# Router logits from the residual's sums, with norm and modulation folded into the router's weights and two rows, and the first pair's rows gathered one token tile at a time

## The chip, the core and the metric

The kernel runs on one core of a Trainium2 chip. The time is that of one execution on the device in microseconds (us); the median of 3 runs stands for it. The rows below come from one profiled execution of the same program. In them PE is TensorE's matmuls, PEld its weight loads, DVE is VectorE, ACT is ScalarE, POOL is GpSimd, SP is the engine whose queue issues nearly all transfers.

## The reference, cut to what matters

One transformer block on 256 tokens of width 1024: a mixer (attention, gated linear attention, pooling), then a mixture of 32 experts of which each token takes 4.

```python
h = x * (1.0 + scale1) + shift1
y = hybrid_mixer(h, ...)                                   # ends in  concat @ w_out
x = layer_norm(ALPHA * x + (1.0 + gate1) * y, ln1_g, ln1_b)
h = x * (1.0 + scale2) + shift2                            # six rows of cond @ w_ada + b_ada
logits = h @ w_router + b_router                           # 1024 -> 32
top_logit, top_e = lax.top_k(logits, 4)
gate = softmax(top_logit)
# each expert: clamped_swiglu(h_rows @ w_gate_up[e] + b) @ w_down[e] + b, weighted by gate, summed per token
x = layer_norm(ALPHA * x + (1.0 + gate2) * y, ln2_g, ln2_b)
```

With r the residual's sum before the first norm, mu and s its mean and inverse deviation of a token, and h = n * hA + hB for the normed row n = (r - mu) * s (hA = ln1_g * (1 + scale2), hB = ln1_b * (1 + scale2) + shift2), the logits are s * (r @ (hA * W)) - mu * s * (sum of hA * W) + (sum of hB * W) + b_router. That is the identity that the change uses.

## The kernel before

The tokens stand in two tiles (t = 0, 1) of 128. The program is a straight list of operations; a scheduler at build time sets the order on each engine, and each engine then runs its own list strictly in order, waiting on semaphores.

**The mixer.** Attention, the linear attention and the pool fill `oT`, the mixer's output with the features on the partitions, in eight blocks k. For attention each head's probabilities `sc` are transposed on PE (`ppT`, lines 560 and 562), copied by ACT to `pT` and multiplied into `po`; DVE copies `po` to `oT` (line 569). Then `py[t][n]` = oT @ w_out is accumulated in four banks, blocks 0, 1, 2, 6, 7 first and the linear attention's blocks 3, 4, 5 at the end.

**Rows of w_ada.** scale2 and shift2 are needed as columns (`m2`): DVE multiplies eight row blocks by cond and adds them up (`accm`, line 546, two sums j = 0, 1 of eight steps), PE adds over the partitions (`pcol`, eight small matmuls for each j), and DVE makes `hA` and `hB` (lines 550 to 553). The rows of gate1 (`acc`) and gate2 (`g2p`) are added up the same way (lines 622 and 624), from tiles `adag`.

**Norm and router, for each t.** DVE makes the residual in place in `n` (the tile n1), its statistics and the inverse deviation; ACT and DVE write the normed row (lines 667 and 668). PE transposes it (`ph`), ACT and DVE modulate it into `h2T` (lines 680 and 682), PE makes the logits on 32 partitions (`plg`), DVE adds the bias, PE turns them back (`plt`). Top-4, the experts' one-hot sum `msel` and the slot numbers `posm` follow (lines 691 to 702).

**The experts.** They are taken in 16 pairs, each expert with 64 slots. `dispatch` builds a one-hot matrix `pp` from `posm`, PE gathers the pair's rows with it (`pxg`), DVE and ACT modulate them into `xg`. `gate_up` multiplies them with four weight tiles `g` of 2 MB, `down` with two tiles `d` of 2 MB.

**The ring.** All large weights go through a ring of five buffers of 2 MB, and from the experts on through three more (`ring2`) that lie where the mixer's tiles were. `adag`, `wo` (two tiles of w_out; wo1 holds the blocks 7, 3, 4, 5) and the first expert tiles `g` follow each other in it. SP issues each load when the tile that held the buffer has had its last reader; its queue is in order too, so a load that waits holds back those behind it. The fifth expert tile takes the buffer of wo1, whose last reader is the last matmul of `py`; the three of `ring2` stand behind it.

Of the kernel before, what the change touches and what calls it, by code (L numbers as in the profile page):

```python
# [112 lines left out]
def block_kernel(ctx: ExitStack, tc, x, w_ada, w_in, gla_w_a2, pool_w, w_out, w_router, w_gate_up, b_gate_up,  # L113
# [57 lines left out]
    def layer_norm_stats(st, pool, name):  # L171
# [4 lines left out]
        return mv[:, 0:1], rs  # L176


    with tc.tile_pool(name="early", bufs=1) as ea, tc.tile_pool(name="late", bufs=1, side="right") as la_, \
# [189 lines left out]
        z2 = la_.tile([P, TT, ZN - O_GV], F32, name="z2")  # L369
# [44 lines left out]
        gaT = ea.tile([RANK, S], F32, name="gaT")  # L414
# [177 lines left out]
        o_gla = la_.tile([P, TT, GVW], F32, name="o_gla")  # L592
# [60 lines left out]
        oh = []  # L653
        for t in range(TT):
            st6 = la_.tile([P, 2, 6], F32, tag="st", name=f"st{t}")
            for n in range(2):
# [414 lines left out]
```

## Time and profile before

| | us |
|---|---|
| median of 3 runs (1127.11 to 1131.95) | 1128.25 |
| the profiled execution, as timed | 1129.8 |
| its span, first to last instruction | 1128.0 |
| PE busy (matmuls; their ends are modelled) | 1035.4 |
| DVE, ACT, POOL busy | 318.7, 98.8, 41.5 |

A busy time is a sum over stages with different limits; it doesn't say which engine sets the end. The transfers of 449.49 MB took 398 GB/s over the span. The stages are the mixer (to about 150 us), norm and router (150 to 187 us) and the experts (187 us to the end).

### The profile page before, as it was taken

The page shows a single profiled execution, that of the slowest core. Times are in us where ns is not written, and L with a number is a line of the kernel's source. Part 1 is how long each engine was busy: PE and PEld are TensorE (multiplying, and loading weights), DVE is VectorE, ACT ScalarE, POOL GpSimd, SP SyncE. Part 2 cuts the span into 40 slices and gives each one's busy share as a digit, 9 for nine tenths or more (in the row PEclk, how much of TensorE's full clock was granted, in tenths as well). Part 3 has the DMA queues.
Part 4 walks back from the last instruction along what each step waited for, and adds up shares of the span by engine and source line. Part 5 has one row for each costly group of instructions (what it writes and reads, how often), then busy time and mean ns, then how long its engine had stood idle before and what let it go on. Part 6 is the DMA issues. An engine that isn't in the chain of part 4 may idle for free.

```text
span 1128.0 us, 11046 instructions
## 1 busy us (share of the span) xinstructions
PE 1035.4 (92%) x4734; PEld 436.9 (39%) x4735; DVE 318.7 (28%) x587; ACT 98.8 (9%) x205; POOL 41.5 (4%) x43
## 2 busy tenths in 40 slices
PE   6999998999999999996999999989989898989795
PEld 3656545434333333333344343423333333333231
DVE  1459694322222122211122221213221121211113
ACT  1024112100000000000000000000000000000100
POOL 2270000000000000000000000000000000000000
PEclk9999897999999999998999999999999999999998
DMA  9997499999999999999899999999999999999992
GB/s 324 348 385 283 181 378 373 428 423 428 428 428 427 428 428 428 428 427 423 344 427 428 428 428 426 428 427 428 428 428 427 428 429 427 428 427 428 428 414 92
DMA packets 52998, 449.49 MB, mean 398 GB/s; under 512 B 5056, under 2 KB 18768, under 8 KB 28496
## 3 DMA queue, kind: packets, MB, share of 16 engines
q1 hardware_dynamic: 52320, 447.90, 95.7%
q8 instruction: 39, 0.64, 0.2%
q10 hardware_dynamic: 624, 0.83, 0.2%
q14 instruction: 15, 0.12, 0.0%
HBM read 447.67 MB, written 1.05 MB: 398 GB/s over the span
## 4 chain that ended last, share of the span: by engine, by line
PE 29%; DMA 22%; DVE 1%; issue 1%; ACT 0%; POOL 0%; DVEq 0%; POOLq 0%
DMA d<-in_w_down 22%; PE gu L134 13%; PE py L134 7%; PE pxg L134 4%; PE ya L134 3%; PE pyl L134 1%; PE paT L837 1%; DVE yb L855 0%; DVE aT L839 0%; DVE res L919 0%; ACT n L931 0%; PE pln L134 0%; DVE r L1038 0%; DVE yl L1015 0%; DVE st L1019 0%
## 5 line engine op out<-in xcount | busy, mean ns | idle before, releaser
L134 PE MATMUL gu<-g,xg 128*64 128x512 f32 x2048 | 462.5, 595 | 14.0 <-DMA g<-in_w_gate_up 12.6
L134 PEld LDWEIGHTS gu<-g,xg 128*64 128x64 f32 x2048 | 143.2, 137 | 295.5 <-issue 261.0
L134 PE MATMUL py<-d,aT 128*64 128x512 f32 x992 | 227.1, 600 | 13.8 <-DMA d<-in_w_down 12.5
L825 DVE TENSOR_SCALAR g<-gu 128x512 f32<-128x512 f32 x32 | 22.1, 692 | 410.1 <-PE gu L134 410.1
L134 PEld LDWEIGHTS py<-d,aT 128*64 128x64 f32 x992 | 70.0, 137 | 150.5 <-issue 140.8
L134 PE MATMUL pxg<-pp,n 128*128 128x128 f32 x512 | 77.0, 302 | 14.9 <-DVE aT L839 7.0
L134 PEld LDWEIGHTS pxg<-pp,n 128*128 128x128 f32 x512 | 69.2, 208 | 43.0 <-issue 29.6
L855 DVE TENSOR_TENSOR yb<-py,g2p 64x512 f32<-64x512 f32 x60 | 41.3, 689 | 139.0 <-PE py L134 138.4
L134 PE MATMUL ya<-yb,sg_None 128*128 128x512 f32 x120 | 58.2, 607 | 4.9 <-DVE yb L855 4.8
L829 ACT ACTIVATE s<-g 128x512 f32<-128x512 f32 x32 | 20.2, 630 | 464.4 <-DVE g L825 464.4
L793 DVE TENSOR_SCALAR xg<-pxg,hA,hB 128x128 f32<-128x128 f32 x64 | 25.8, 409 | 99.2 <-PE pxg L134 90.0
L791 ACT ACTIVATE xg<-pxg,hB,hA 128x128 f32<-128x128 f32 x64 | 28.7, 457 | 274.3 <-DVE xg L793 273.6
L134 PE MATMUL pz<-wz,hT 128*128 128x512 f32 (+2 forms) x128 | 52.4, 547 | 0.0
L169 POOL TENSOR_TENSOR rsb<-rtb,half 128x2 f32<-128x2 f32 x1 | 0.7, 701 | 950.9 <-DVE rtb L168 950.9
L839 DVE COPY aT<-paT 128x512 f32<-128x512 f32 x32 | 22.1, 692 | 43.9 <-PE paT L837 43.8
L134 PE MATMUL py<-wo,oT 128*128 128x512 f32 x64 | 30.9, 629 | 0.2 <-ACT oT L642 0.2
L134 PEld LDWEIGHTS ya<-yb,sg_None 128*128 128x128 f32 x120 | 20.4, 189 | 26.9 <-issue 17.4
L134 PEld LDWEIGHTS pz<-wz,hT 128*128 128x128 f32 x128 | 23.4, 190 | 17.3 <-issue 14.3
L837 PEld LDWEIGHTS paT<-kc,l 128*128 128x128 f32 x128 | 18.0, 209 | 25.3 <-DVE l L831 15.4
L837 PE MATMUL paT<-kc,l 128*128 128x128 f32 x128 | 23.7, 308 | 0.0
L831 DVE TENSOR_TENSOR l<-l,s 128x512 f32<-128x512 f32 x32 | 22.1, 691 | 3.4 <-DVE l L830 0.5
L134 PE MATMUL pqk<-hT,wz 128*128 128x256 f32 x96 | 22.2, 381 | 0.7 <-DVE hT L332 0.7
(245 smaller groups left out, 519.1 us busy)
## 6 DMA issues: line engine op xcount, KB each, us to landing
g<-in_w_gate_up SPq DMA_DIRECT2D x128, 2048.0 KB, 30.4
d<-in_w_down SPq DMA_DIRECT2D x62, 2048.0 KB, 30.4
adam<-in_w_ada SPq DMA_DIRECT2D x4, 2048.0 KB, 16.7
adag<-in_w_ada SPq DMA_DIRECT2D x4, 2048.0 KB, 9.0
ada<-in_w_ada SPq DMA_DIRECT2D x6, 1024.0 KB, 11.1
wz<-in_w_in SPq DMA_DIRECT2D x8, 760.0 KB, 9.5
wo<-in_w_out SPq DMA_DIRECT2D x2, 1536.0 KB, 10.0
ada<-in_w_ada SPq DMA_DIRECT2D x4, 512.0 KB, 7.4
```

Of the source, the lines that this page charges most:

```text
L134: T.matmul(o, l, r, start=start, stop=stop, skip_group_check=True, **kw)
L169: G.tensor_tensor(o, t[:, :n], half[:, :n], op=OP.pow)
L791: A.activation(xg[:, k], bs[k // 4][:, k % 4], AF.Identity, bias=hB[:, k:k + 1], scale=hA[:, k:k + 1])
L793: V.tensor_scalar(xg[:, k], bs[k // 4][:, k % 4], hA[:, k:k + 1], hB[:, k:k + 1], op0=OP.mult, op1=OP.add)
L825: V.tensor_scalar(g, gu[:, 0], LIMIT, None, op0=OP.min)
L829: A.activation(s, g, AF.Sigmoid, scale=SW_ALPHA)
L831: V.tensor_mul(l, l, s)
L837: T.transpose(b[:, j], act[:, j::4], ident)
L839: V.tensor_copy(aT, b)
L855: V.tensor_mul(yb[m * CAP:(m + 1) * CAP, n * 512:(n + 1) * 512], b[r], g2p[r, n * 512:(n + 1) * 512])
```

## The change

The router no longer waits for the norm. The router's weights are multiplied by hA and by hB once (`wr2`), summed over the partitions and the eight blocks (`wrs`, PE `prow`) into two rows `rrow`; that code stands right behind hA and hB. In the loop over t each half of the residual is transposed as soon as it is made, copied by ACT to `h2T` unmodulated, and the logits come out on 128 partitions from `h2T` as the stationary operand and `wr2` of 32 columns; one DVE instruction applies the deviation and adds the row. The first pair's one-hot matrix is built and its rows are gathered in the loop, tile by tile (`pxgA`, in two banks that `py` had), and modulated into `xgA`, a buffer that the even pairs then use; the odd ones have the other. Some tiles share space differently: the 4 KB of `xgA` stand in the part of SBUF that lives through the whole program, `gaT` shares with `pm`, `z2` is split, and `o_gla` takes the place of `z_gr`.

```diff
+    xgA = const.tile([P, KT, P], F32, name="xgA")
...
+    def one_hot(pp, pcol, t):
+
+        V.tensor_tensor(pp[:, t], pcol[:, t, :, None].to_broadcast([P, 2, CAP]),
+                        iota1[:, None, :].to_broadcast([P, 2, CAP]), op=OP.is_equal)
+
+    def gathered(bs, pp, t):
+
+        for k in range(KT):
+            mm(bs[k // 4][:, k % 4], twos(n1[:, t], k), pp[:, t].rearrange("p a s -> p (a s)"),
+               t == 0 and k % 4 == 0, t == TT - 1)
+
+    def modulated(xg, bs):
+        for k in range(KT):
+            if k % 2:
+                A.activation(xg[:, k], bs[k // 4][:, k % 4], AF.Identity, bias=hB[:, k:k + 1], scale=hA[:, k:k + 1])
+            else:
+                V.tensor_scalar(xg[:, k], bs[k // 4][:, k % 4], hA[:, k:k + 1], hB[:, k:k + 1], op0=OP.mult, op1=OP.add)
...
+        wr2 = la_.tile([P, 2, KT, NE], F32, tag="qin", name="wr2")
+        for j, h in enumerate((hA, hB)):
+            V.tensor_mul(wr2[:, j], wr, h[:, :, None].to_broadcast([P, KT, NE]))
+        wrs = la_.tile([P, 2, NE], F32, name="wrs")
+        V.tensor_reduce(wrs, wr2.rearrange("p j k e -> p j e k"), axis=AX.X, op=OP.add)
+        b = bank("prow")
+        mm(b[:, 0:2 * NE], ones, wrs.rearrange("p j e -> p (j e)"), True, False)
+        mm(b[:, NE:2 * NE], colv[:, 80:81].to_broadcast([P, P]), kc[:, K_I4:K_I4 + NE], False, True)
+        rrow = la_.tile([P, 2, NE], F32, name="rrow")
+        V.tensor_copy(rrow, b[:, 0:2 * NE].rearrange("p (j e) -> p j e", j=2))
...
                 V.bn_stats(st6[:, n], y)
+                b = bank(f"ph{t}{n}").rearrange("p (j s) -> p j s", j=4)
+                for j in range(4):
+                    T.transpose(b[:, j], twos(xs[:, t], 4 * n + j), ident)
+                A.copy(h2T[:, 4 * n:4 * n + 4, t * P:(t + 1) * P], b)
             mu, rs = layer_norm_stats(st6, la_, f"a{t}")
             nmr = la_.tile([P, 1], F32, tag="nmr", name=f"nmr{t}")
             V.scalar_tensor_tensor(nmr, mu, -1.0, rs, op0=OP.mult, op1=OP.mult)
+            row = la_.tile([P, NE], F32, tag="row", name=f"row{t}")
+            V.scalar_tensor_tensor(row, rrow[:, 0], nmr, rrow[:, 1], op0=OP.mult, op1=OP.add)
+            b = bank(f"plg{t}")
+            for k in range(KT):
+                mm(b[:, 0:NE], h2T[:, k, t * P:(t + 1) * P], wr2[:, 0, k], k == 0, k == KT - 1)
+            V.scalar_tensor_tensor(lg[:, t], b[:, 0:NE], rs, row, op0=OP.mult, op1=OP.add)
...
-            for q in range(2):
-                b = bank(f"ph{t}{q}").rearrange("p (j s) -> p j s", j=4)
-                for j in range(4):
-                    k = 4 * q + j
-                    T.transpose(b[:, j], twos(n1[:, t], k), ident)
-                for j in range(4):
-                    k = 4 * q + j
-                    o = h2T[:, k, t * P:(t + 1) * P]
-                    if j % 2:
-                        A.activation(o, b[:, j], AF.Identity, bias=hB[:, k:k + 1], scale=hA[:, k:k + 1])
-                    else:
-                        V.tensor_scalar(o, b[:, j], hA[:, k:k + 1], hB[:, k:k + 1], op0=OP.mult, op1=OP.add)
-            b = bank(f"plg{t}")
-            for k in range(KT):
-                g = slice(32 * (k // 2), 32 * (k // 2) + 32)
-                mm(b[g, :P], wr[:, k], h2T[:, k, t * P:(t + 1) * P], k % 2 == 0, k % 2 == 1)
-            V.tensor_scalar(lgp[:, t * P:(t + 1) * P], b[:, :P], colv[:, 80:81], None, op0=OP.add)
-            b = bank(f"plt{t}")
-            mm(b[:, 0:NE], lgp[:, t * P:(t + 1) * P], kc[:, K_I4:K_I4 + NE], True, True)
-            V.tensor_copy(lg[:, t], b[:, 0:NE])
...
             V.scalar_tensor_tensor(posm[:, t], b[:, 0:NE], 1.0, msel[:, t], op0=OP.add, op1=OP.mult)
+            one_hot(ppA, posm[:, :, 0:2], t)
+            if t == 0:
+                first = [bank(f"pxgA{q}", "z").rearrange("p (j s) -> p j s", j=4) for q in range(2)]
+            gathered(first, ppA, t)
+        modulated(xgA, first)
...
+        if nm == "0":
+            xg = xgA
+        else:
+            xg = xgA if nm in evens else wk.tile([P, KT, P], F32, tag="xg", name=f"xg{nm}", bufs=1)
+            bs = [mps.tile([P, 4, P], F32, tag="m", name=f"pxg{nm}_{q}") for q in range(2)]
```

The scheduler moves instructions with it; three places are shown. The first is PE's list between the linear attention's transposes and the attention's output, in the program at the end of `pz` (the last part of w_in). Before:

```order
L134 MATMUL pcol_645<-kc,accm_636 128x4 x8
L560 MATMUL ppT_678<-kc,sc_508 128x128
L562 MATMUL ppT_678<-kc,sc_509 128x128 x2
L134 MATMUL po_677<-pT_682,z_397 64x256
...
L134 MATMUL kv_742<-z_398,kout 128x192
L134 MATMUL pcol_664<-kc,accm_655 128x4 x8
L134 MATMUL py_841<-wo_158,oT 128x512
```

And with the change:

```order
L134 MATMUL pcol_647<-kc,accm_638 128x4 x8
L134 MATMUL pcol_666<-kc,accm_657 128x4 x8
L134 MATMUL prow<-wrs,kc 128x64
L134 MATMUL prow<-kc,colv 128x32
L592 MATMUL ppT_690<-kc,sc_510 128x128
L594 MATMUL ppT_690<-kc,sc_511 128x128 x2
L134 MATMUL po_689<-pT_694,z_398 64x256
```

The second `pcol` (of the sum accm with j = 1) stood behind all of the attention's output, and now stands with `prow` ahead of its first transpose. The second place is DVE's list at the same point of the program, from the first result of `pcol` (`m`) on. Before:

```order
L550 TENSOR_TENSOR m_635<-pcol_645,colv 128x8
L546 SCALAR_TENSOR_TENSOR accm_655<-adam_0_154,cond,accm_655 128x1024
L546 SCALAR_TENSOR_TENSOR accm_655<-adam_1_156,cond,accm_655 128x1024
L574 TENSOR_TENSOR sg<-sg,z_398 128x768
L546 SCALAR_TENSOR_TENSOR accm_655<-adam_1_156,cond,accm_655 128x1024
L569 COPY oT<-po_677 128x256
L546 SCALAR_TENSOR_TENSOR accm_655<-adam_1_156,cond,accm_655 128x1024
L569 COPY oT<-po_695 128x256
L546 SCALAR_TENSOR_TENSOR accm_655<-adam_1_156,cond,accm_655 128x1024
```

And with the change (`sg` is the gate of the linear attention, `acc` the sum for gate1):

```order
L569 TENSOR_TENSOR m_637<-pcol_647,colv 128x8
L565 SCALAR_TENSOR_TENSOR accm_657<-adam_0_155,cond,accm_657 128x1024
L565 SCALAR_TENSOR_TENSOR accm_657<-adam_1_157,cond,accm_657 128x1024
L606 TENSOR_TENSOR sg<-sg,z_gr 128x768
L565 SCALAR_TENSOR_TENSOR accm_657<-adam_1_157,cond,accm_657 128x1024
L607 TENSOR_TENSOR sg<-sg,zb 128x768
L565 SCALAR_TENSOR_TENSOR accm_657<-adam_1_157,cond,accm_657 128x1024 x2
L569 TENSOR_TENSOR m_637<-pcol_666,colv 128x8
L570 TENSOR_TENSOR hA<-m_637,colv 128x8
L571 TENSOR_TENSOR hB<-m_637,colv 128x8
L578 TENSOR_TENSOR wr_679<-wr,hA 128x256
```

The copies of `po` moved behind the sums and the new products. The third place is PE's list from the last matmuls of `py` to the first expert. With the change it reads (`py_851` and `py_852` are the banks of t = 1):

```order
L698 MATMUL ph_916<-kc,n_65 128x128 x4
L134 MATMUL plg_932<-wr_679,h2T 128x32 x4
L134 MATMUL py_851<-wo_162,oT 128x512
L134 MATMUL plg_932<-wr_679,h2T 128x32 x4
L134 MATMUL py_852<-wo_162,oT 128x512 x3
L134 MATMUL ppos_950<-msel,kc 128x32
L698 MATMUL ph_972<-kc,n_65 128x128 x4
L698 MATMUL ph_985<-kc,n_65 128x128 x2
L134 MATMUL pxgA_954<-ppA,n_65 128x128 x4
L134 MATMUL pxgA_955<-ppA,n_65 128x128 x4
```

Before, every `py` matmul stood ahead of the first `ph`; now the first tile's transposes and logits stand ahead of the last `py`, and half of the first gather stands ahead of the second tile's logits.

## Rows read from the trace of the kernel before

**Rows 1.** The page: the span.

```profile
span 1128.0 us, 11046 instructions
```

**Rows 2.** Busy time by stretch, from and to; the last number is GB/s moved.

```profile
200.00:300.00 100.00, 96.73 (x466) 38.66 (x464) 25.16 (x47) 7.19 (x15) 0.00 (x0) 1.00 1.01 427
...
600.00:1128.00 528.00, 475.75 (x2181) 179.52 (x2180) 116.16 (x204) 32.27 (x64) 2.11 (x2) 0.99 0.97 409
```

**Rows 3.** The same view, around the expert tiles' first refill.

```profile
188.00:190.00 2.00, 2.00 (x12) 0.72 (x10) 0.86 (x4) 1.85 (x4) 0.00 (x0) 1.00 0.66 279
190.00:192.00 2.00, 2.00 (x14) 0.59 (x10) 0.00 (x0) 0.47 (x1) 0.00 (x0) 1.00 0.33 82
192.00:194.00 2.00, 2.00 (x12) 0.68 (x10) 0.00 (x0) 0.00 (x0) 0.00 (x0) 1.00 0.76 229
194.00:196.00 2.00, 2.00 (x14) 0.83 (x12) 0.00 (x0) 0.00 (x0) 0.00 (x0) 1.00 1.03 442
```

**Rows 4.** Timeline of SP's queue: start, length, line, load, count.

```profile
147.09 0.34 SPq L737 DMA_DIRECT2D g<-in_w_gate_up  x1
...
164.54 1.98 SPq L737 DMA_DIRECT2D g<-in_w_gate_up  x4
...
190.91 3.76 SPq L742 DMA_DIRECT2D d<-in_w_down  x2
```

**Rows 5.** Timeline of PE, attention's output: start, length; in brackets idle time and its end.

```profile
107.68 1.94 PE L134 MATMUL pcol<-kc,accm 128*128 128x4 f32 x16
...
109.47 0.31 PE L560 MATMUL ppT<-kc,sc 128*128 128x128 f32 x1
...
113.09 1.25 PE L134 MATMUL po<-pT,z 128*64 128x256 f32 x8 [0.85 <-ACT pT L564]
...
119.09 2.48 PE L134 MATMUL pcol<-kc,accm 128*128 128x4 f32 x16
...
121.44 2.05 PE L134 MATMUL py<-wo,oT 128*128 128x512 f32 x2
```

**Rows 6.** Timeline of DVE, the sums accm.

```profile
109.65 0.17 DVE L550 TENSOR_TENSOR m<-pcol,colv 128x8 f32<-128x8 f32 x1 [0.23 <-PE pcol L134]
...
109.74 2.59 DVE L546 SCALAR_TENSOR_TENSOR accm<-adam,cond,accm 128x1024 f32<-128x1024 f32 x2
...
112.70 0.96 DVE L574 TENSOR_TENSOR sg<-sg,z 128x768 f32<-128x768 f32 x1 [0.37 <-ACT sg L573]
...
116.68 1.28 DVE L546 SCALAR_TENSOR_TENSOR accm<-adam,cond,accm 128x1024 f32<-128x1024 f32 x1
```

**Rows 7.** Timeline of DVE, prices for the new products and reduction.

```profile
94.89 0.95 DVE L487 TENSOR_REDUCE mx<-sc 128x6 f32<-128x768 f32 x1
...
101.67 0.55 DVE L514 TENSOR_TENSOR kin<-z,tmp 128x384 f32<-128x384 f32 x1
...
132.78 0.55 DVE L612 TENSOR_REDUCE ms<-sq 128x4 f32<-128x384 f32 x1 [2.85 <-ACT sq L610]
```

**Rows 8.** Timeline of PE, from the last of py to the first expert.

```profile
153.94 10.57 PE L134 MATMUL py<-wo,oT 128*128 128x512 f32 x24 [0.24 <-ACT oT L642]
...
165.17 1.22 PE L675 MATMUL ph<-kc,n 128*128 128x128 f32 x8 [0.67 <-ACT n L667]
...
172.58 1.95 PE L675 MATMUL ph<-kc,n 128*128 128x128 f32 x8
...
181.59 5.69 PE L134 MATMUL pxg<-pp,n 128*128 128x128 f32 x32
...
187.21 7.09 PE L134 MATMUL gu<-g,xg 128*64 128x512 f32 x32
```

**Rows 9.** Busy time by stretch; the number ahead of the DMA share is the granted clock.

```profile
120.00:121.00 1.00, 1.00 (x8) 1.00 (x8) 0.00 (x0) 0.00 (x0) 0.00 (x0) 0.74 0.85 270
...
127.00:128.00 1.00, 1.00 (x10) 0.70 (x7) 0.49 (x2) 0.00 (x0) 0.00 (x0) 0.85 0.03 12
```

**Rows 10.** Timeline of PE, the last matmul run with a wait before pair 6.

```profile
510.29 3.65 PE L134 MATMUL py<-d,aT 128*64 128x512 f32 x16 [1.16 <-DMA d<-in_w_down]
```

More of the change, by code (lines that the diff above doesn't have):

```diff
@@ L368, in block_kernel @@
         z1 = ea.tile([P, TT, O_GV], F32, name="z1")
-        z2 = la_.tile([P, TT, ZN - O_GV], F32, name="z2")
+        z_gv = la_.tile([P, TT, GVW], F32, name="z_gv")
+        z_gr = la_.tile([P, TT, GVW], F32, tag="gr", name="z_gr")
         a = W1 - C_FV
@@ L407, in second_part @@
                     V.tensor_add(z1[:, t, O_GA - o:O_GA], b[:, :o], zb[:, O_GA - o:O_GA])
-                    V.tensor_add(z2[:, t, 0:GVW], b[:, o:c1 - c0], zb[:, O_GV:O_GR])
+                    V.tensor_add(z_gv[:, t], b[:, o:c1 - c0], zb[:, O_GV:O_GR])
                 else:
-                    V.tensor_add(z2[:, t, GVW:], b[:, :c1 - c0], zb[:, O_GR:ZN])
+                    V.tensor_add(z_gr[:, t], b[:, :c1 - c0], zb[:, O_GR:ZN])
         lin = ea.tile([P, TT, FH + GKW], F32, name="lin")
-        gaT = ea.tile([RANK, S], F32, name="gaT")
+        gaT = ea.tile([P, 2, S], F32, tag="pm", name="gaT")[0:RANK, 0]
         b = bank("gaT")
@@ L591, in block_kernel @@
                                            op0=OP.mult, op1=OP.add)
-        o_gla = la_.tile([P, TT, GVW], F32, name="o_gla")
+        o_gla = la_.tile([P, TT, GVW], F32, tag="gr", name="o_gla")
         for t in range(TT):
@@ L643, in block_kernel @@
         h2T = la_.tile([P, KT, S], F32, tag="hT", name="h2T")
-        lgp = la_.tile([P, S], F32, tag="qin", name="lgp")
         lg = la_.tile([P, TT, NE], F32, name="lg")
@@ L653, in block_kernel @@
         oh = []
+        ppA = la_.tile([P, TT, 2, CAP], F32, tag="kin", name="ppA")
         for t in range(TT):
@@ L774, in weights @@
         return loaded.pop((kind, e))
+    evens = [str(i) for i in range(0, NE // 2, 2)]
     def dispatch(pcol, gcol, nm):
@@ L780, in dispatch @@
         for t in range(TT):
-            V.tensor_tensor(pp[:, t], pcol[:, t, :, None].to_broadcast([P, 2, CAP]),
-                            iota1[:, None, :].to_broadcast([P, 2, CAP]), op=OP.is_equal)
-        xg = wk.tile([P, KT, P], F32, tag="xg", name=f"xg{nm}")
-        bs = [mps.tile([P, 4, P], F32, tag="m", name=f"pxg{nm}_{q}") for q in range(2)]
-        for t in range(TT):
-            for k in range(KT):
-                mm(bs[k // 4][:, k % 4], twos(n1[:, t], k), pp[:, t].rearrange("p a s -> p (a s)"),
-                   t == 0 and k % 4 == 0, t == TT - 1)
-        for k in range(KT):
-            if k % 2:
-                A.activation(xg[:, k], bs[k // 4][:, k % 4], AF.Identity, bias=hB[:, k:k + 1], scale=hA[:, k:k + 1])
-            else:
-                V.tensor_scalar(xg[:, k], bs[k // 4][:, k % 4], hA[:, k:k + 1], hB[:, k:k + 1], op0=OP.mult, op1=OP.add)
+            one_hot(pp, pcol, t)
+        if nm == "0":
[3 more added lines that the diff above has]
+            bs = [mps.tile([P, 4, P], F32, tag="m", name=f"pxg{nm}_{q}") for q in range(2)]
+            for t in range(TT):
+                gathered(bs, pp, t)
+            modulated(xg, bs)
         def gates(m=None):
@@ L1027, in block_kernel @@
     stats = [(mv[:, t, 0:1], rs[:, t:t + 1]) for t in range(TT)]
-    r = [wk.tile([P, D], F32, tag="xg", name=f"r{t}") for t in range(TT)]
+    r = [xgA.rearrange("p k s -> p (k s)"), wk.tile([P, D], F32, tag="xg", name="r1", bufs=1)]
     for t in range(TT):
```

2 lines of the change are left out of this document (removed).

## Prediction, made before the changed kernel ran

> **What bounds the kernel now.** I read the busy time by stretch first. From 200 us to the end the transfers run at 427 and 409 GB/s [rows 2] while PE is busy for 97 and 90% of the stretch: the experts' stage is a stream of weight tiles that nearly never pauses, and PE is only a little faster than it. So the end comes when the stream ends, and the stream ends early or late by what it lost before 200 us. The reader should look for its last pause. It is at 188 to 194 us: three stretches of 2 us at 279, 82 and 229 GB/s [rows 3], by the even rate 3.2 us lost. The timeline of SP's queue says why: the eight buffers were full, and the next load, the first tile `d`, was issued at 190.91 [rows 4], 3.70 us after PE began the first expert at 187.21 [rows 8], when the first tile `g` had been read. Bytes flowed again 2.0 us after the issue (458 KB until 194, about 1.1 us at the even rate, so from 192.9). This is the anchor: **before, the first `d` tile starts to flow at 192.9.**
>
> A second reading of the same rows matters more here. The fifth to eighth `g` are issued together at 164.54 [rows 4], 0.03 us after the last matmul of `py` ends (153.94 + 10.57 = 164.51 [rows 8]). They hang on the buffer of wo1. So two conditions hold for the first `d`: PE must have begun the first expert 3.7 us earlier, and four tiles of 2.097 MB, each 4.9 us at 427 GB/s, must have flowed since the end of `py`. Before, the second asks only for 164.5 + 2.0 + 19.6 = 186.1 (with what then still stood in the queue about 190), so the first decides. It has 6.8 us of room.
>
> Does a later stream show at the end? Before the sixth pair, where all engines meet, PE waits for `d` by 1.16 us [rows 10]: it has just caught up with the transfers there. A later stream is therefore handed on in full, and a later start of PE but for some 1 us.
>
> **The change at the front of PE's list.** The second `pcol` and `prow` now stand ahead of the attention's output. I add up when they can run.
>
> - DVE: `m` at 109.65 (0.17); then five steps of accm at 1.28 to 1.30 (a pair takes 2.59) and two products of 768 at 0.96 [rows 6], the second of the shape of the first: 109.65 + 0.17 + 6.45 + 1.92 = 118.2. Before, the sum was done at 116.68 + 1.28 = 117.96, with three copies among it: DVE gains nothing, but before nobody waited, since the attention's output ran meanwhile.
> - PE: from 109.6 to 118.2 it has nothing to do. Then `pcol`, 1.94 at the full and 2.48 with part of it at the low clock [rows 5]; I take 2.4: 120.6.
> - DVE: `m`, hA, hB at about 0.17 each, two products of 256 elements (no row; between 0.17 for the smallest and 0.55 for 384 [rows 7], taken as 0.42, nearer the latter), the reduction of 512 (between 0.55 for 384 and 0.95 for 768, taken as 0.68): 2.0, bounds 1.5 to 2.6: 122.6.
> - PE: `prow`, two small matmuls like two of the sixteen records' eight in `pcol` (0.3 each) and a latency: 0.8: **the first `ppT` at 123.4 instead of 109.47, 13.9 us later.**
>
> The scale `wr2` itself, the split of `z2` and the shared buffers cost nothing beyond this: their DVE work is in the sum or takes the place of equal work. The copy to `rrow` (0.2 us) lies beside PE's transposes.
>
> **From there to the end of `py`.** Before: 109.47 to 164.51, 55.0 us. Out of it go the second `pcol` (119.09 to 121.44, 2.35) and the wait of 0.85 at 113.09 for ACT [rows 5], whose table load for the gate now comes in PE's pause. Into it come the first tile's eight transposes, 1.22 [rows 8], and its logits, eight matmuls with 128 columns of weights and little to stream, like a `pcol`, 1.94 (bounds 1.2 and 2.5, transposes at full clock and `pcol` at the low one). 55.0 - 3.2 + 3.2 = 55.0, so **`py` ends at 178.4**, 13.9 us later than before.
>
> The clock needs a choice. Before, it fell at 120.5 (0.74 over the stretch of 120 to 121) and rose at 127.3 (0.85 over 127 to 128 [rows 9]), 6.8 us at half speed inside this piece, after a piece in which PE had waited by bits. With a pause of 8.6 us I take it that it falls in the pause and is low for as long after `ppT` starts, to about 130: the same loss, no term. The Trainium skill, "TensorE: Matmul & The Clock Gate", section "Why this matters for your kernels", says that a gap between bursts of matmuls takes the clock back to its low level; by it the fall comes in the new pause, ahead of `pcol`, and not after it, and what it leaves open is when it rises. [...]
>
> **The router.** After `py`, before, PE needed 22.7 us to the first expert (164.51 to 187.21). The first tile's share of it, up to the second tile's transposes at 172.58 [rows 8], 8.1 us, now lies beside `py`; half of the gather (5.69 / 2 = 2.8) is ahead too, but partly in this piece still. So 22.7 - 8.1 - 2.8 = 11.8 at best and 14.6 at worst, that is, PE starts the first expert at 190.2 to 193.0. The router's chain is really some 8 to 11 us shorter; the front has eaten it.
>
> **The sum.** Condition one: 190.2 to 193.0 + 3.7 + 2.0 = 195.9 to 198.7. Condition two: 178.4 + 2.0 + 19.6 = 200.0. The second now decides: **200.0 - 192.9 = 7.1 us later.** The loads ahead of these four don't help: DVE can begin `acc` at about 124 instead of 129, and the transfers that follow it come some us earlier, but then the queue stands still until wo1 is free. PE's own delay (3.0 to 5.8, less 1) stays under 7.1. The profiled execution took 1129.8 for a span of 1128.0 [rows 1], so 1.8 lie around the span and stay; it would take 1129.8 + 7.1 = 1136.9. It is 1.55 above the median of the runs, which becomes 1128.25 + 7.1 = **1135.4 us**. A measurement of this kernel can tell about 0.5%, 5.6 us, from no change; this is a little over it.
>
> **The rivals.**
>
> 1. *The front costs less.* The clock may stay high or rise at once when the transposes begin; before it stayed high through waits of 0.5 to 1 us, up to 120.5. Then the 6.8 us at half speed go: 3.4 us less, `py` ends at 175.0, condition two gives 196.6, condition one about 192.5 to 195.3: 3.7 us later, 1132.0. For it: nothing in the rows shows the clock after a pause in this stage. Against it: it fell after much smaller gaps.
> 2. *The router wins.* The change does what the shorter chain suggests if PE's pause at the front comes to nothing. The point that decides: `py` must end by 192.9 - 21.6 = 171.3, so the front may cost 6.8 us. With none of it, `py` ends at 164.5, the first expert starts at about 176 to 179, condition two gives 186.1 + 0.03 and condition one at best 182 to 185, with what stands in the queue 189 to 190: 3 to 4 us earlier, 1124.7. For it: the chain from residual to first gather is the only long stretch in which PE is starved. Against it: the list of PE is strict, and DVE's five steps can't be done before 116.
> 3. *The clock stays low.* `ppT` and `po` wait for ACT's copies (0.85 and more in [rows 5]). If the clock stays low through them, until the matmuls of `py` follow each other at about 137, another 6.8 us run at half speed: 3.4 us more, 10.5 later, 1138.8. [...] For it: in [rows 9] it rose only when PE had worked without gaps. Against it: waits of this size alone did not hold it down ahead of 119.
>
> **How the numbers follow.** Forecast (6 to 9 us later) 0.52; rival 1 (2 to 6 later) 0.24; rival 2 0.09; rival 3 (9 to 12 later) 0.15. The range must leave no more than 0.2 out: rival 2 and half of rival 3 fall outside 1130.5 to 1139.5, about 0.16. The bounds of the unknown prices (0.5 us each way for DVE's products, 0.7 for the logits) are inside it. Slower by over 0.5% (over 1133.9): rival 3, most of the forecast (0.44): 0.59. Faster by over 0.5% (under 1122.6): only if rival 2 were larger than worked out: 0.03. The rest 0.38.
>
> **What would show it.** Right: a pause of PE of 8 to 9 us from about 109.6 and another of 2 us before `prow`; first `ppT` at 122.5 to 124.5; last `py` at 175 to 181; four `g` issued together just then; transfers that stand still between the fourth and the fifth `g` for 4 us or more, and none at 188 to 194; first expert at 189 to 194. From 200 us on all as before, some 7 us later. Wrong: if the first `ppT` comes before 117 (rival 2), if the fifth `g` doesn't wait for `py`, or if PE meets full buffers and the first `d` again waits for it, so that the stream is no longer what is late.

## The result, and the profile after

| | before | changed |
|---|---|---|
| median of 6 runs each | 1129.39 | 1137.51 |
| span of the profiled execution | 1128.0 | 1134.8 |
| ratio, 95% interval | | 1.0070 [1.0043, 1.0097] |

The change makes the kernel slower by 0.7%: 8.1 us by the medians, 4.9 to 11.0 by the interval, 6.8 by the spans. Forecast were 7.1 and 1135.4.

The timeline of PE, for the place of [rows 5] (start, length, group; in brackets the idle time ahead of it and what ended it):

```profile
107.95 1.94 PE L134 MATMUL pcol<-kc,accm 128*128 128x4 f32 x16
118.11 3.58 PE L134 MATMUL pcol<-kc,accm 128*128 128x4 f32 x16 [8.22 <-DVE accm L565]
124.28 0.66 PE L134 MATMUL prow<-wrs,kc 128*128 128x64 f32 x2 [2.60 <-DVE wrs L580]
...
125.13 0.45 PE L592 MATMUL ppT<-kc,sc 128*128 128x128 f32 x1
```

PE stands still for 8.22 us and again for 2.60, and the attention's output begins at 125.13 instead of 109.47. DVE, at the place of [rows 6], shows what it waits for:

```profile
115.45 2.60 DVE L565 SCALAR_TENSOR_TENSOR accm<-adam,cond,accm 128x1024 f32<-128x1024 f32 x2
121.73 0.17 DVE L569 TENSOR_TENSOR m<-pcol,colv 128x8 f32<-128x8 f32 x1 [3.67 <-PE pcol L134]
...
122.13 0.43 DVE L578 TENSOR_TENSOR wr<-wr,hA 128x256 f32<-128x256 f32 x1
...
123.13 1.01 DVE L580 TENSOR_REDUCE wrs<-wr 128x64 f32<-128x512 f32 x1
```

The sum is done at 118.05, as early as before; the work between the two PE rows is 2.4 us. PE's end of `py` and the first expert, for [rows 8]:

```profile
175.03 2.82 PE L134 MATMUL py<-wo,oT 128*128 128x512 f32 x6
178.06 0.38 PE L134 MATMUL ppos<-msel,kc 128*128 128x32 f32 x2 [0.21 <-DVE msel L719]
...
179.76 2.05 PE L134 MATMUL pxgA<-ppA,n 128*128 128x128 f32 x16
...
187.39 3.78 PE L134 MATMUL pxgA<-ppA,n 128*128 128x128 f32 x16
191.10 7.46 PE L134 MATMUL gu<-g,xgA 128*64 128x512 f32 x32
```

`py` ends at 177.85 instead of 164.51. SP's queue, for [rows 4]:

```profile
163.56 0.33 SPq L764 DMA_DIRECT2D g<-in_w_gate_up  x1
...
177.88 1.93 SPq L764 DMA_DIRECT2D g<-in_w_gate_up  x4
195.17 3.76 SPq L769 DMA_DIRECT2D d<-in_w_down  x2
```

The four `g` go together 0.03 us after the end of `py`, 14.3 us after the one ahead of them. What that does to the transfers is in the busy time by stretch (as [rows 3] and [rows 9]: span, busy time of PE, PEld, DVE, ACT and POOL, granted clock, DMA share, GB/s):

```profile
112.00:114.00 2.00, 0.00 (x0) 0.00 (x0) 2.00 (x3) 0.00 (x0) 0.00 (x0) 0.85 1.02 420
114.00:116.00 2.00, 0.00 (x0) 0.00 (x0) 2.00 (x3) 0.00 (x0) 0.00 (x0) 0.50 1.03 422
128.00:130.00 2.00, 2.00 (x8) 1.43 (x8) 0.00 (x0) 0.79 (x2) 0.00 (x0) 0.50 0.00 0
130.00:132.00 2.00, 2.00 (x15) 1.74 (x14) 1.13 (x2) 0.42 (x2) 0.00 (x0) 0.89 0.00 0
132.00:137.00 5.00, 5.00 (x25) 2.32 (x24) 4.40 (x7) 1.09 (x3) 0.00 (x0) 1.00 0.13 17
174.00:176.00 2.00, 2.00 (x12) 1.30 (x11) 1.88 (x6) 1.94 (x2) 0.00 (x0) 1.00 0.76 324
176.00:178.00 2.00, 1.85 (x5) 0.54 (x3) 1.93 (x10) 0.39 (x2) 0.00 (x0) 1.00 0.02 8
178.00:180.00 2.00, 1.47 (x11) 1.34 (x11) 2.00 (x5) 0.59 (x1) 0.00 (x0) 1.00 0.77 156
188.00:190.00 2.00, 2.00 (x11) 2.00 (x11) 0.45 (x2) 0.05 (x1) 0.00 (x0) 0.50 0.98 418
190.00:192.00 2.00, 2.00 (x10) 1.22 (x11) 0.79 (x3) 0.43 (x2) 0.00 (x0) 0.53 0.98 406
192.00:194.00 2.00, 2.00 (x12) 0.66 (x10) 2.00 (x11) 0.79 (x2) 0.00 (x0) 1.00 0.96 399
```

The pause of the stream has moved: it stands at 176 to 178 (8 GB/s), and at 188 to 194, where it stood before, 399 to 418 GB/s flow. With the partly filled rows on both sides it costs 3.7 us at 427 GB/s, so it is a little shorter than the 4 us or more that were foretold. The first five rows show the clock: it falls to the low level in PE's pause and rises between 130 and 132. What the stream has lost can be counted over the 100 us from the start of the first `pcol`, before and with the change:

```profile
107.68:207.68 100.00, 92.59 (x407) 50.51 (x407) 65.68 (x134) 17.77 (x34) 5.07 (x4) 0.90 0.80 319
...
107.95:207.95 100.00, 85.74 (x389) 50.34 (x388) 61.54 (x126) 15.03 (x28) 5.02 (x4) 0.88 0.74 287
```

That is 31.9 MB before and 28.7 MB with the change; the 3.2 MB between them take 7.5 us at 427 GB/s. The last wait of PE for `d` before the sixth pair, which answers to [rows 10], and a group of that pair's first expert:

```profile
517.33 3.65 PE L134 MATMUL py<-d,aT 128*64 128x512 f32 x16 [1.16 <-DMA d<-in_w_down]
...
556.15 1.90 PE L134 MATMUL gu<-g,xgA 128*64 128x512 f32 x6 [1.07 <-issue]
```

The wait is the same 1.16 us, 7.04 later. The second group stood at 549.24 before:

```profile
549.24 1.90 PE L134 MATMUL gu<-g,xg 128*64 128x512 f32 x6 [1.07 <-issue]
```

From there to the end both take the same, 578.76 and 578.65. So in these two profiles all of the loss is made before 200 us and carried through the experts.

### The profile page after: what moved, and what is told of

It reads as the page before. It is cut to its first block, busy times and chain, and to the rows that moved or that the text cites. A ratio compares the mean times of both kernels' runs of the same rounds, so it can differ in the third digit from the quotient of the medians.

```text
span 1134.8 us, 11048 instructions
## 1 busy us (share of the span) xinstructions
PE 1034.0 (91%) x4734; PEld 442.3 (39%) x4735; DVE 318.5 (28%) x585; ACT 97.7 (9%) x201; POOL 41.3 (4%) x43
## 4 chain that ended last, share of the span: by engine, by line
PE 29%; DMA 22%; DVE 1%; issue 1%; ACT 0%; POOL 0%; DVEq 0%; POOLq 0%
DMA d<-in_w_down 22%; PE gu L134 13%; PE py L134 7%; PE pxg L134 4%; PE ya L134 3%; PE pyl L134 1%; PE paT L862 1%; DVE yb L880 0%; DVE aT L864 0%; DVE res L944 0%; ACT n L956 0%; PE pln L134 0%; PE pl L134 0%; DVE yl L1040 0%; DVE xgA L1063 0%
## 5 line engine op out<-in xcount | busy, mean ns | idle before, releaser
L134 PE MATMUL gu<-g,xgA 128*64 128x512 f32 x1024 | 231.9, 596 | 7.2 <-DMA g<-in_w_gate_up 6.1
L134 PE MATMUL gu<-g,xg 128*64 128x512 f32 x1024 | 232.2, 596 | 6.8 <-DMA g<-in_w_gate_up 6.8
L134 PEld LDWEIGHTS py<-d,aT 128*64 128x64 f32 x992 | 73.8, 137 | 148.6 <-issue 138.7
L134 PEld LDWEIGHTS gu<-g,xg 128*64 128x64 f32 x1024 | 71.7, 136 | 149.3 <-issue 130.9
L134 PEld LDWEIGHTS gu<-g,xgA 128*64 128x64 f32 x1024 | 71.9, 137 | 147.8 <-issue 129.9
L134 PE MATMUL pxg<-pp,n 128*128 128x128 f32 x480 | 71.4, 298 | 14.6 <-DVE aT L864 7.1
L134 PEld LDWEIGHTS pxg<-pp,n 128*128 128x128 f32 x480 | 64.0, 205 | 42.4 <-issue 29.9
L862 PEld LDWEIGHTS paT<-kc,l 128*128 128x128 f32 x128 | 18.0, 209 | 25.3 <-DVE l L856 14.6
L196 DVE TENSOR_SCALAR xgA<-pxg,hA,hB 128x128 f32<-128x128 f32 x28 | 11.3, 409 | 51.3 <-PE pxg L134 47.1
L196 DVE TENSOR_SCALAR xg<-pxg,hA,hB 128x128 f32<-128x128 f32 x32 | 12.9, 409 | 44.9 <-PE pxg L134 40.0
L194 ACT ACTIVATE xgA<-pxg,hB,hA 128x128 f32<-128x128 f32 x28 | 12.6, 457 | 147.4 <-DVE xgA L196 147.1
```

Of the source, the lines that this page charges most:

```text
L134: T.matmul(o, l, r, start=start, stop=stop, skip_group_check=True, **kw)
L194: A.activation(xg[:, k], bs[k // 4][:, k % 4], AF.Identity, bias=hB[:, k:k + 1], scale=hA[:, k:k + 1])
L196: V.tensor_scalar(xg[:, k], bs[k // 4][:, k % 4], hA[:, k:k + 1], hB[:, k:k + 1], op0=OP.mult, op1=OP.add)
L862: T.transpose(b[:, j], act[:, j::4], ident)
```

## The experiments

Executions differ by some 4 us before they come to the changed places: the first `pcol` began between 107.5 and 111.8 in the twelve profiles, with the same work ahead of it. So the marks below are counted from its start, each the start (for `py` the end) of a row like those above; "pair 6" is the group with the wait of 1.07. What follows pair 6 isn't equal in all kernels: from there to the end the twelve profiles take between 576.2 and 582.0 us, so a step at pair 6 needn't be the step at the end. Each row of marks is one profile. The last column compares the times of all runs with runs of before on the same chip, whose median was 1127.4 beside kernels 1 to 4 and 1128.6 beside 5 to 10 and the second "changed".

| kernel | first ppT | py's end | first expert | first d issued | pair 6 | median | ratio to before |
|---|---|---|---|---|---|---|---|
| before | 1.8 | 56.8 | 79.5 | 83.2 | 441.6 | 1129.4 | |
| changed | 17.2 | 69.9 | 83.2 | 87.2 | 448.2 | 1137.5 | 1.0070 [1.0043, 1.0097] |
| changed, again | 17.2 | 70.7 | 83.9 | 88.4 | 449.5 | 1137.1 | 1.0077 [1.0041, 1.0113] |
| 1 fold later | 1.8 | 60.0 | 76.6 | 80.5 | 438.5 | 1128.3 | 0.9989 [0.9966, 1.0012] |
| 2 fold unused, in before | 17.2 | 68.4 | 89.5 | 93.2 | 451.7 | 1139.6 | 1.0093 [1.0062, 1.0125] |
| 3 later buffers ahead of wo1's | 17.2 | 70.5 | 83.8 | 88.2 | 446.8 | 1135.0 | 1.0050 [1.0028, 1.0071] |
| 4 both, 1 and 3 | 1.8 | 60.7 | 75.9 | 80.6 | 438.6 | 1127.2 | 0.9982 [0.9962, 1.0002] |
| 5 filler in the pause | 15.7 | 68.1 | 81.4 | 85.4 | 443.1 | 1136.0 | 1.0060 [1.0035, 1.0085] |
| 6 fold later, gather as before | 1.8 | 58.9 | 73.4 | 77.1 | 439.6 | 1128.3 | 0.9988 [0.9965, 1.0010] |
| 7 all edits | 1.8 | 62.3 | 72.7 | 76.4 | 439.7 | 1129.9 | 0.9995 [0.9970, 1.0020] |
| 9 all edits, later buffers first | 1.8 | 57.6 | 70.9 | 74.6 | 432.2 | 1120.1 | 0.9945 [0.9921, 0.9969] |
| 10 as 9, on 4 | 1.8 | 58.9 | 69.4 | 73.1 | 432.8 | 1123.4 | 0.9947 [0.9926, 0.9967] |

**1. The front undone.** The fold's code moves behind the attention's output; nothing else changes.

```diff
-        wr2 = la_.tile([P, 2, KT, NE], F32, tag="qin", name="wr2")
...
-        V.tensor_copy(rrow, b[:, 0:2 * NE].rearrange("p (j e) -> p j e", j=2))
         for m in range(3):
             po = bank(f"po{m}")
...
+        wr2 = la_.tile([P, 2, KT, NE], F32, tag="qin", name="wr2")
...
+        V.tensor_copy(rrow, b[:, 0:2 * NE].rearrange("p (j e) -> p j e", j=2))
         sg = ea.tile([P, TT, GVW], F32, tag="kz", name="sg")
```

> The changed kernel with the fold (wr2, wrs, prow, rrow) written behind the attention's output instead of ahead of it; all of the computation stays. In the order on PE the second pcol and prow then stand behind the last po, as the second pcol did before. Theory F (the front): PE's pause ahead of the attention's output is the whole loss, because it makes py end late and four g tiles hang on that end. Then the first ppT comes at 109 to 110, py ends at 166 to 169 (164.5 of before and some 3 for the first tile's transposes and logits), the first expert starts at 177 to 181, the first d tile flows at 189 to 190 instead of 199.5, and the time is 1125 to 1127, some 11 below the changed kernel. Rival T (the tail): the loss is made at the end of py, by the transposes, logits and half a gather that now stand among its matmuls, and the pause at the front would have been absorbed: 1135 to 1138. Rival X (the experts): the loss is in the experts, by the two xg buffers of one each: 1135 to 1138 with the front restored.

PE's timeline:

```profile
109.57 0.31 PE L581 MATMUL ppT<-kc,sc 128*128 128x128 f32 x1
...
172.09 3.76 PE L134 MATMUL pxgA<-ppA,n 128*128 128x128 f32 x16
175.65 1.75 PE L134 MATMUL plg<-wr,h2T 128*128 128x32 f32 x8
...
184.38 7.25 PE L134 MATMUL gu<-g,xgA 128*64 128x512 f32 x32
```

`ppT`, the end of `py` (167.72) and the four `g` (167.75) come as the theory of the front says, and the loss is gone: 9.2 us less than the changed kernel by the medians, 9.7 at pair 6 (some 11 were expected, and a time of 1125 to 1127, where 1128.3 was measured). Both rivals expected 1135 or more, so neither the end of `py` nor the new buffers of the experts make the loss. The first expert is a miss: 184.38 instead of 177 to 181. In PE's list half a gather stands ahead of the second half of the second tile's logits, and ran at the low clock (3.76 against 2.05); DVE waited for those logits:

```profile
177.44 0.25 DVE L708 SCALAR_TENSOR_TENSOR lg<-plg,rsa,row 128x32 f32<-128x32 f32 x1 [4.80 <-PE plg L134]
```

Against before the gain is 3.1 us at pair 6, of which the times can tell nothing (0.9989, interval across 1).

**2. The front alone.** The kernel before with the same lines of the fold added ahead of the attention's output, and nothing that uses `rrow`.

```diff
+        wr2 = la_.tile([P, 2, KT, NE], F32, tag="qin", name="wr2")
...
+        V.tensor_copy(rrow, b[:, 0:2 * NE].rearrange("p (j e) -> p j e", j=2))
         for m in range(3):
             po = bank(f"po{m}")
```

> The kernel before with the fold's operations (wr2, wrs, prow, rrow) added ahead of the attention's output and their result not used; norm, router and gather are those of before. In the order on PE the second pcol and prow stand ahead of the first ppT, as in the changed kernel. Theory F: PE pauses as in the changed kernel, py ends at 174 to 176, the old router needs 22.7 us from there, so the first expert starts at 197 to 199 and the first d tile flows 6 us later, at 203 to 205: 10 to 12 us later than before, 1139 to 1142, slower than the changed kernel too; the difference to the changed kernel (2 to 5) is what the shorter router gives there. Rivals T and X: the tail and the experts are those of before, so the time is that of before within 2 us, 1128 to 1132.

```profile
118.00 3.58 PE L134 MATMUL pcol<-kc,accm 128*128 128x4 f32 x16 [8.22 <-DVE accm L546]
...
191.71 5.70 PE L134 MATMUL pxg<-pp,n 128*128 128x128 f32 x32
197.34 7.09 PE L134 MATMUL gu<-g,xg 128*64 128x512 f32 x32
```

The pause is the same 8.22 us, and this kernel has the longest median: 10.1 us later than before at pair 6, 0.93% by the times. Against before this is clear; against the changed kernel the intervals overlap. It also prices the router: with the same front the first expert starts 6.3 us later than in the changed kernel (89.5 against 83.2; 5.6 by that one's second profile), of which 3.5 (2.2) are left at pair 6.

**3. Which condition holds the first `d`.** One line: the fifth to seventh tile go to the later buffers, and only the eighth waits for wo1.

```diff
-            i = int(turn[0] % (NA + NB) >= NA)
+            i = int(NA - 1 <= turn[0] % (NA + NB) < NA + NB - 1)
```

> The changed kernel with one line changed: the three later buffers come round after the fourth buffer of the first five instead of after the fifth, so that the fifth to seventh g go into them and only the eighth hangs on wo1 and so on the end of py. Theory F, with the step that the four tiles behind the end of py decide and not the start of the first expert: the transfers don't stand still at 176 to 178, the eighth g is through at 177.9 + 2 + 4.9 = 185, and the first d waits for the first expert alone: 191.1 + 4.1 + 2.0 = 197.2 instead of 199.5, so 2.3 us faster than the changed kernel, 1135. Rival G (the first expert's start decides in the changed kernel already, and the queue behind py is only a companion): no change, 1137.5. If the three buffers come free late as well, the four tiles are issued together again and nothing is learnt.

```profile
176.00:180.00 4.00, 4.00 (x26) 3.04 (x26) 3.15 (x10) 2.68 (x3) 0.55 (x1) 1.00 0.99 422
180.00:184.00 4.00, 3.32 (x16) 1.88 (x15) 3.93 (x15) 0.98 (x3) 0.00 (x0) 1.00 1.01 428
```

(This profile began 3.4 us late; its `py` ends at 181.8, so the two stretches are where the changed kernel's transfers stood still.) The pause is gone though `py` ends no earlier: the one-line edit removes it, so it hung on wo1's buffer and the end of `py`. Pair 6 comes 1.4 earlier than in the changed kernel's first profile and 2.6 than in its second, the median 2.5 and 2.1: about what was forecast. The size isn't shown, though. The intervals of the times overlap, and the profile is that of the longest of the 12 executions (1140.5 us): from the first `pcol` to the end it takes 1027.2 us, no less than the changed kernel's two, 1026.9 and 1026.6.

**4. Both edits.** The diffs of 1 and 3 together.

> Both edits: the fold behind the attention's output, and the three later buffers ahead of the fifth. Theory F: the first expert starts at 177 to 181, so the first d may flow from 183 to 187, but eight tiles of 4.9 us stand ahead of it, which flowed until 188 to 189 before; the stream then has no pause after 150, the time is 1124 to 1126, and the second edit gives 0 to 1.5 us on top of the first. Rivals T and X: 1133 to 1138.

No step over the first at pair 6 (438.6 against 438.5), within the 0 to 1.5 expected; rivals T and X fall again. The time, 1127.2, is a miss against the 1124 to 1126 expected, and so is the first expert, at 183.4 instead of 177 to 181.

**5. The clock's part.** The changed kernel, with matmuls on the identity ahead of the second `pcol`.

```diff
+            if j:
+                b = bank("fill")
+                for i in range(30):
+                    mm(b[:, 0:P], ident, ident, True, True)
             b = bank(f"pcol{j}", "z")[:, 0:32].rearrange("p (q m) -> p q m", q=8)
```

> The changed kernel with 30 matmuls of 128 x 128 ahead of the second pcol, into a bank that nobody reads, so that PE works through the pause of 109.9 to 118.1 (some 7.7 us by pxgA's 0.128 each at full clock, two records a matmul). Theory C: the low clock that the pause leaves behind (0.50 from 113 to 130.9) costs some 4 us of the changed kernel's loss. Then the granted clock stays at 1.00 up to 118 at least, the second pcol takes 1.94 instead of 3.58, the first ppT comes at 123 instead of 125.1, py ends at 173 to 175 instead of 177.9, and the time is 3 to 4.5 us below the changed kernel, 1133 to 1134.5 where that takes 1137.5. If the clock falls all the same at 120, as it did before without a pause, 1.5 to 2.5 are won. Rival N: the half speed is hidden behind ACT's copies and DVE; py ends at 177 to 178 and the time is the changed kernel's within 1 us. Even at the full clock the pause itself stays, so the time stays above before by 3 or more.

```profile
116.00:120.00 4.00, 4.00 (x38) 4.00 (x37) 4.00 (x5) 0.00 (x0) 0.00 (x0) 1.00 1.03 419
120.00:124.00 4.00, 2.55 (x21) 2.27 (x19) 1.83 (x2) 0.00 (x0) 0.00 (x0) 1.00 1.03 404
124.00:128.00 4.00, 1.44 (x7) 1.35 (x7) 2.53 (x8) 0.00 (x0) 0.00 (x0) 0.69 0.99 390
128.00:132.00 4.00, 3.43 (x13) 2.10 (x12) 0.00 (x0) 0.99 (x3) 0.00 (x0) 0.50 0.35 139
```

The filler took 6.94 us and left a wait of 1.42 ahead of the second `pcol`. The clock stayed at its high level through both, and that `pcol` took 2.05 us instead of 3.58; then it fell all the same, in the wait of 2.60 for `wrs`, and was low until 132. `py` ends 1.8 to 2.6 earlier than in the two profiles of the changed kernel. At pair 6 the gain is 5.1 to 6.4 us, more than any step explains, but this profile loses most of it again behind that mark: it takes 581.96 us from there to the end, where the changed kernel's two take 578.65 and 577.19. From the first `pcol` to the end it is 1.8 and 1.6 us shorter than they are, and in the 100 us from the first `pcol` it moves 29.4 MB against 28.7 and 28.4, which is 1.6 to 2.3 us at 427 GB/s. By the times the gain is 1.1 to 1.5, with overlapping intervals. So the part of the low clock that the filler removed is worth some 1 to 2.5 us, about what was expected for a clock that falls all the same (1.5 to 2.5), and below the 3 to 4.5 of theory C. The pause itself is the larger part: the filled kernel is still 0.6% slower than before.

**6. The gather as before.** Experiment 1, with the lines of the gather taken out of the loop and the first pair gathered behind the router like the others.

```diff
-            one_hot(ppA, posm[:, :, 0:2], t)
...
-            gathered(first, ppA, t)
-        modulated(xgA, first)
```

> The fold behind the attention's output, as in the first experiment, and the first pair's gather as before: all of it behind the router. Theory P (PE is what the router's end waits for): half a gather ahead gains nothing, since it stands in PE's list in front of the second tile's logits, for which DVE waited 4.80 us in the first experiment. Then the logits come some 3.7 earlier, the whole gather 32 records long behind them, and the first expert starts at 183 to 186 (184.4 in the first experiment): the time is that of the first experiment within 1.5 us, 1125 to 1129. Rival Q: the half gather ahead is a gain of 2.8 or more: the first expert starts at 187 to 188.5, d flows 3 later, and the time is 2 to 3.5 above the first experiment's, 1129 to 1132.

```profile
174.52 1.06 PE L134 MATMUL plg<-wr,h2T 128*128 128x32 f32 x8
...
179.03 5.91 PE L134 MATMUL pxg<-pp,n 128*128 128x128 f32 x32
```

The first expert starts 3.2 us earlier than in the first experiment (73.4 against 76.6), some 2 us earlier than expected, so rival Q falls: the half gather ahead is no gain. That its place costs something is not shown. Of the 3.2 us, 1.0 is there at the end of `py` already (58.9 against 60.0), ahead of any gather. Behind it, experiment 1 ran half a gather and the second half of the logits at the low clock (3.76 and 1.75 us, granted clock 0.50 from 172 to 184), where 2.05 and 1.06 were measured at the high one: 2.4 us, as much as the 2.2 that are left. The time is the same (1128.3 both), so here an earlier first expert didn't show at the end.

**7. All that this points to.** Fold behind the `kv` matmuls, later buffers ahead of the fifth, half the gather behind the second tile's logits, and the first four steps of the gate1 sum written earlier.

```diff
+        acc1 = la_.tile([P, D], F32, tag="acc", name="acc1")
+        V.tensor_scalar(acc1, ada_g1[0][:, 0], cond[:, 0:1], None, op0=OP.mult)
+        for k in range(1, 4):
+            V.scalar_tensor_tensor(acc1, ada_g1[0][:, k], cond[:, k:k + 1], acc1, op0=OP.mult, op1=OP.add)
...
+            if t:
+                first = [bank(f"pxgA{q}", "z").rearrange("p (j s) -> p j s", j=4) for q in range(2)]
+                gathered(first, ppA, 0)
             A.activation(n1[:, t, 0:512], xs[:, t, 0:512], AF.Identity, bias=nmr, scale=rs)
```

> All that the runs so far point to, on the changed kernel: the fold behind the kv matmuls, the three later buffers ahead of the fifth, the first half of the gather behind the second tile's logits, and the first four steps of the sum for gate1 written ahead of the linear attention, so that the last adag load is issued at some 133 instead of 139. Theory F: the transfers then run ahead of PE, the first expert starts at 180 to 183 and the first d waits for it alone: 180 to 183 + 4 + 2 = 186 to 189 against 192.9 of before, 4 to 7 us earlier than before and 1 to 2.5 below the fold moved by itself: 1122 to 1125 where before takes 1128. Rival: the sums that move forward on DVE make the linear attention late by as much, py ends after 170 and nothing is won over the fourth experiment: 1125 to 1128.

A miss: the first expert comes 6.8 us earlier than before and 3.9 earlier than in experiment 1, and pair 6 only 1.9 earlier than before and 1.2 later than in experiment 1; the time is that of before, 1129.9 instead of 1122 to 1125. The stream offers a reason:

```profile
140.00:144.00 4.00, 4.00 (x23) 2.74 (x23) 2.71 (x5) 0.49 (x1) 0.26 (x1) 1.00 0.44 117
144.00:148.00 4.00, 4.00 (x29) 2.43 (x27) 3.07 (x4) 0.00 (x0) 1.74 (x1) 1.00 0.99 407
148.00:152.00 4.00, 4.00 (x12) 1.85 (x11) 3.07 (x4) 0.49 (x1) 1.40 (x1) 1.00 0.01 3
```

The last `adag` was issued at 141.07 and the first `g`, which waits for the end of the gate1 sum, at 151.72; between the two only that `adag` flows, and then nothing. Counted from the first `pcol` the first `g` goes at 40.4, where it went at 39.6 in experiment 1. What PE wins at the router is then no use, since the tiles aren't there sooner. `py` too ends later than in experiment 4 (62.3 against 60.7), as the rival has it; four edits are made at once here, and no run separates them.

**8. The changed kernel again.**

> The changed kernel again, unchanged, so that the others of this call have it beside them on the same chip: 1136 to 1139, 7 to 10 above before. With the first expert at 191.1 and the first tile d issued 4.1 later, as in its first profile.

1137.1, as in the table.

**9 and 10. The stream's start.** The later buffers come first, so the first three `g` wait for no gate sum; 9 on kernel 7 (whose lists of PE, DVE and ACT stay the same), 10 on kernel 4 with half the gather behind the logits.

```diff
-            i = int(NA - 1 <= turn[0] % (NA + NB) < NA + NB - 1)
+            i = int(turn[0] % (NA + NB) < NB)
```

> The kernel with all edits (the fold behind kv, half the gather behind the second tile's logits, the gate1 sum begun earlier), but with the three later buffers taken first of all: the first three g go into them and the last five into the five of the ring. All lists of PE, DVE and ACT stay as they are. Theory S (only the stream of weights counts now, not the first expert): with all edits PE began the first expert 72.7 us after its first pcol instead of 79.5, and that gave nothing, because the queue stood still from 137 to 141 and 148 to 152 for a sum on DVE; the first g then no longer waits for that sum. It follows the last adag at once (30 us after the first pcol instead of 40), the second g goes when the linear attention's gate has been read, at 43, so eight tiles are through at 43 + 2 + 7 x 4.9 = 79 instead of 83 to 85, PE asks for the first d at 73 + 4 + 2 = 79 as well: 3 to 4.5 us earlier than with all edits, 1123 to 1125 where before takes 1128. Rival: the stream's late start is not it, and the experts run at a pace of their own: no change, 1128 to 1130.

> The same buffer order on the fourth kernel (fold behind the attention's output), with half the gather behind the second tile's logits and the gate1 sum left where it was. The last adag is issued 31.5 us after the first pcol, the first g behind it, the second g when the linear attention's gate has been read, at 41; eight tiles are through at 41 + 2 + 34.3 = 77, and the first expert starts at 74 to 76 as in the fourth experiment or 2 earlier, so the first d flows at 79.7 to 82. Theory S: 2.5 to 4.5 us below the fourth experiment, 1123 to 1125 where before takes 1128, and PE is what is late again. Rival: no change.

SP's queue and the same stretches of kernel 9:

```profile
132.70 0.37 SPq L234 DMA_DIRECT2D adag<-in_w_ada  x1
133.60 32.01 SPq L772 DMA_DIRECT2D g<-in_w_gate_up  x8
182.31 3.76 SPq L777 DMA_DIRECT2D d<-in_w_down  x2
```

```profile
136.00:140.00 4.00, 4.00 (x28) 2.55 (x27) 2.70 (x4) 0.26 (x1) 1.37 (x1) 1.00 1.06 436
140.00:144.00 4.00, 4.00 (x10) 1.71 (x9) 3.07 (x4) 0.23 (x1) 1.77 (x1) 1.00 1.05 447
144.00:148.00 4.00, 4.00 (x12) 1.82 (x11) 3.77 (x6) 0.00 (x0) 0.20 (x1) 1.00 0.33 78
```

The first `g` follows the last `adag` by 0.9 us; the second waits, and the stream still pauses at 144 to 148. Pair 6 comes 7.5 us earlier than in kernel 7, by 4.5 expected at most, and the two profiles differ by more than the edit: with the same lists on PE, DVE and ACT, kernel 9 issued the last `adag` 25.0 us after the first `pcol` and ended `py` at 57.6, kernel 7 at 29.7 and 62.3; its clock was low (0.50 over 126 to 134, where kernel 9 had 1.00). From the end of `py` to the first expert it is the other way round: 10.46 us in kernel 7, 13.37 in kernel 9. The stretch of 168 to 176, in kernel 7 and then in kernel 9:

```profile
168.00:176.00 8.00, 6.85 (x38) 4.59 (x36) 6.73 (x22) 3.35 (x6) 0.55 (x1) 1.00 1.00 427
...
168.00:176.00 8.00, 7.93 (x41) 7.82 (x41) 3.70 (x20) 1.63 (x4) 0.56 (x1) 0.57 1.02 434
```

So the edit's price comes from the times: 0.9945 against 0.9995, on two chips, each beside runs of before; the intervals just don't meet. For kernel 10, pair 6 comes 5.8 us earlier than in kernel 4 (2.5 to 4.5 expected), the time, 1123.4, is as expected, and the first expert, at 69.4 instead of 74 to 76, is a miss; it differs from kernel 4 by two edits. Kernel 9 is faster than before by 0.55% (0.31 to 0.79), and kernel 10 by 0.53%; both are some 1.2% faster than the changed kernel. That the router's gain reaches the end once the tiles are there for it is argued and not shown: the buffer order was not run on the kernel before, without the router's change, and by itself it may give part of the gain. Against that speaks only that the first `d` waited for the first expert there, and not for the tiles ahead of it.

## Why the prediction was right

**The front.** Foreseen were a pause of 8.6 us and one of 2 ahead of `prow`; they were 8.22 and 2.60. The first `ppT` came at 125.13 instead of 123.4, and two terms of that sum were too small: the second `pcol`, taken at 2.4, ran wholly at the low clock (3.58), and DVE's products with the reduction took 2.4 instead of 2.0 (the reduction 1.01, outside my bounds of 0.55 to 0.95).

**From there to the end of `py`.** 52.7 us instead of 55.0, so `py` ended at 177.85 against 178.4 forecast. The front came out 1.7 us too late and this piece 2.3 too short: the two errors cancel by luck. Most of the 2.3 is in the trace. The clock was low for 5.3 us after the first `ppT`, where I took 6.8, and in 0.57 of them PE only waited: some 1.0 us. PE was idle for 0.94 us, where the sum leaves 1.24 (2.09 before, less the wait of 0.85): 0.3. The first tile's transposes and logits held up the list for 1.08 and 1.63 us instead of 1.22 and 1.94: 0.45. Some 0.5 us stay open.

**The clock.** The choice was that it falls in the pause and is low until about 130: 0.85 in 112 to 114, 0.50 from 114, up again between 130 and 132. The Trainium skill, "TensorE: Matmul & The Clock Gate", section "Why this matters for your kernels", puts the fall into a gap between bursts, and the trace of the changed kernel agrees. A long gap isn't needed, though: before the change, the clock fell at 120.5 although PE's longest wait from 109.5 on was 0.85 us, and in experiment 5 it fell in a wait of 2.60. The third rival, a low clock up to 137, falls (1.00 over 132 to 137). The first rival, that the pause leaves no low clock, falls too.

**The router.** The first expert at 191.10 lies in the 190.2 to 193.0 forecast. From the end of `py` PE takes 13.25 us to it, within the 11.8 to 14.6 forecast and 9.4 less than before, within the 8 to 11. Not all of that is gain: with the front equal (experiment 2) the first expert comes 6.3 us earlier, since `py` ends 1.5 us earlier without the first tile's transposes and logits in its list, and the old router takes 21.1 us there. The sum counted between nothing and 2.8 us for half a gather done ahead; experiment 6 shows no gain from its place.

**The condition that decides.** Four `g` behind the end of `py`, at 177.88, and a stream that stands still there: so it was, and experiment 3 removes the pause without touching `py`. 200.0 - 192.9 = 7.1 us was the sum; 7.04 and 6.9 were measured at pair 6 (6.6 counted from the first `pcol`), 6.8 in the span. That the number is so close owes something to the errors that cancel ahead of the end of `py`; with its measured end the sum gives 199.45.

**The rival on the other side.** That the router wins with the front at nothing is borne out at pair 6 alone: there experiment 1 comes 3.1 us earlier, for 3 to 4 forecast; in the times it is too small to see. The steps to that number were not as forecast: the first expert started at 184.4 and not at 176 to 179, so its size is in part luck. The limit of 6.8 us for the front was not tried; the runs have a front of nothing or of some 14 to 15 us.

## What to carry to other kernels

An edit that shortens a chain can lengthen another by where its operations land in an engine's list: look at the list of the engine that must not wait, at the first place where something new waits for a slower engine, and move the new code behind work that is ready. Where a stream of weights sets the end, ask of each saved microsecond whether the tiles are there for it; a buffer that comes free late holds back all loads behind it in its queue, and the order in which buffers come round is a cheap thing to change. A mark in the middle of a program shows what happened before it; what of it is left at the end has to be read from the times.

## What was unexpected of the hardware

- A `pcol` of 16 records took 1.94 us where PE had been busy, 2.05 behind the filler and its wait of 1.42, and 3.58 behind the pause, at granted clocks of 1.00, 1.00 and 0.50; half a gather took 2.05 and 3.78 in one and the same kernel. Kernels 7 and 9, with the same lists on PE, DVE and ACT, took 10.46 and 13.37 us from the end of `py` to the first expert, at granted clocks of 1.00 and 0.57 over 168 to 176.
- Twelve executions with the same work ahead began the first `pcol` between 107.5 and 111.8, a spread as large as most effects here. The marks counted from it repeat to 1.3 us between the two profiles of the changed kernel, the only kernel with two.
